# RG-LRU gates as 64x64 blocks between the steps of a later projection, in a stage with a written order

## The chip, the cores and the metric

The kernel runs on one core of a Trainium2 chip. The metric is the device time of one execution in microseconds. The core has a matrix engine (TensorE, PE in the profile; PEld is its loading of weights), two engines for element-wise work (VectorE = DVE, ScalarE = ACT), GpSimd (POOL), and SyncE (SP), which here issues all transfers. TensorE writes to eight banks of PSUM, of 512 float32 values per partition each; VectorE and ScalarE read them.

## What is computed

One layer of a diffusion backbone in float32: 1024 latent tokens and 256 context tokens of width 1024 are normalised, modulated, and sent through a mixer and a feed-forward part. The part that matters here is the first half of the mixer:

```
h      = modulate(rms_norm(x), sh1, sc1)
xr, gr, cq, ckv, kr = split(h @ w_in)            # 512 + 512 + 256 + 128 + 32 columns
xc     = depthwise_conv4(xr)                     # along the tokens
r      = sigmoid(block_diag(w_a) xc + b_a)       # 8 heads of 64x64, two directions
i      = sigmoid(block_diag(w_x) xc + b_x)
log_a  = -8 r softplus(-lambda)
u      = sqrt(1 - exp(2 log_a)) * (i * xc)
h_t    = a_t h_(t-1) + u_t                       # forward and backward, context first
y_lru  = (h_fwd + h_bwd) * gelu(gr)
x      = x + gt1 * rms_norm([y_lru, attention(cq, ckv, kr)] @ w_out)
```

The modulation vectors are `silu(c) @ w_mod + b_mod`, six pieces of 1024. Pieces 0 and 1 (sh1, sc1) are needed before the mixer; 3 and 4 (sh2, sc2) after it, in the layout of the features; 2 and 5 (gt1, gt2), the residual gates, as rows.

## The kernel before

Tokens are worked on in 10 tiles of 128 (two of context, eight latent). Matmuls on float32 data go in three terms: every operand is split into a high part and the rest (`split`, lines 78 to 80: a copy on ScalarE or GpSimd, then a subtraction, line 76, on VectorE or GpSimd).

The first stage (to line 466) normalises and transposes the tokens, modulates them (`h_mod`, line 214; its affine is lines 188 to 192), and makes the 416 token-major columns of the projection (`tok_mm`, line 275, 24 matmuls a tile; `tok_out`, line 288). This stage stands inside `tc.manual_schedule()`, which means that each engine, the issuing of transfers on SyncE included, runs its instructions in the order in which the code creates them. It ends at line 466.

The second stage (lines 500 to 679) is ordered by the planner of the language. It makes the eight blocks of 128 feature-major columns (`proj`, line 485). A block is 8 steps k, and a step is three terms (lines 492, 494, 496) for three chunks of 512, 512 and 256 tokens (blocks m = 0 to 3, the recurrent ones) or two of 512 (m = 4 to 7, the gelu ones). The weights come by `load_w` and `prep_w`. After a recurrent block comes `conv` (lines 532 to 537: two reads on ScalarE, six multiply-adds on VectorE). A block's gates (`gate`, line 540) are four products, for two directions and two gates, each with a 128x128 matrix that holds two 64x64 heads on its diagonal and zeros beside them, in plain float32, three chunks each. Sigmoid (line 545), exponential and tanh (`coefs`, lines 565 and 566), and root (line 573) follow on ScalarE, the rest and the scans on VectorE (lines 567 to 591). The planner loads a new function table on ScalarE whenever the function's set changes (ACT_TABLE_LOAD).

Between the projections the later modulation runs as 16 steps (`mod2_step`, line 413): each brings two slices of 512 KB and makes four matmuls on four column tiles (line 424). After four steps the sum is copied and either transposed (line 433) or, for the residual gates, summed into a row (line 436), worked on in four halves (lines 439 to 445) and written to memory, from where `gt_row` spreads it later.

`tok_norm` (line 610) normalises the token-major columns, with a square root on ScalarE inside `rstd_of` (line 102). `ckv_t` (line 631) transposes the key latents in three pieces. Then the attention's operands are made (from line 688), and from line 968 the attention runs in a written order.

Pages come from pools: `R` has 12 pages, `W` five. In the second stage PSUM holds two "big" tiles of three banks and two small ones of one bank ("sm").

Of the kernel before, what the change touches and what calls it, by code (L numbers as in the profile page):

```python
# [34 lines left out]
def hybrid_layer_kernel(ctx: ExitStack, tc: tile.TileContext, A, out):  # L35
# [87 lines left out]
    for h in range(2):  # L123
        V.tensor_tensor(sel2[:, h:h + 1], ident[:, 64 * h:64 * h + 1], ident[:, 64 * h + 32:64 * h + 33], ALU.add)

# [277 lines left out]

    def mod2_load(s):

        n, kp = divmod(s, 4)
        col = (2, 1, 0, 3)[n]
        w2[s] = R(), R()
        for j in range(2):
            k = 2 * kp + j  # L410
            nc.sync.dma_start(out=w2[s][j][:, :D], in_=A["w_mod"][k * 128:(k + 1) * 128, col * 1024:(col + 1) * 1024])

    def mod2_step(s):

        n, kp = divmod(s, 4)
        if s + 1 < 16:
            mod2_load(s + 1)
        if kp == 0:
            acc2[n] = ps_small()
# [6 lines left out]
        if kp == 3:  # L426
            mr = R()
            S.activation(mr[:, 0:512], acc2.pop(n), AF.Copy)
            po = ps_small()
            if n < 2:  # L430
                pt = po[:, 0:8].rearrange("p (m h) -> p m h", h=2)
                for m in range(4):
                    T.matmul(pt[:, m, :], mr[:, m * 128:(m + 1) * 128], sel2, start=True, stop=True)
                V.tensor_copy(mod2[:, n].rearrange("p (h m) -> p m h", h=2), pt)
            else:
                T.matmul(po[0:2, :], sel2, mr[:, 0:512], start=True, stop=True)
                r = 2 * (n - 2)
                rw, gr = (mr[0:2, 512 + 256 * x:768 + 256 * x] for x in range(2))
                for h in range(2):
                    c = slice(h * 256, (h + 1) * 256)  # L440
                    for x, q_ in ((rw, r), (gr, r + 1)):
                        nc.sync.dma_start(out=x, in_=A["rows"][q_:q_ + 1, :].rearrange("o (a b) -> (o a) b", a=2)[:, c])
                    V.tensor_tensor(rw, po[0:2, c], rw, ALU.add)
                    V.tensor_tensor(rw, rw, gr, ALU.mult)
                    nc.sync.dma_start(out=gt_d[n - 2:n - 1, :].rearrange("o (a b) -> (o a) b", a=2)[:, c], in_=rw)
# [5 lines left out]

    for g in range(2, 5):
        if g == 2:
            last_x = load_x(9)
# [30 lines left out]
    def proj(w, chunks, name):  # L485
# [3 lines left out]
        for k in range(8):  # L489
# [10 lines left out]
    nl, sp, z, z2, q = (C([128, 8]) for _ in range(5))  # L500
    V.tensor_scalar(out=nl, in0=P("lam"), scalar1=-1.0, scalar2=None, op0=ALU.mult)
    V.tensor_tensor(z, nl, P("lam"), ALU.max)
    S.activation(z, z, AF.Exp, scale=-1.0)
    V.tensor_scalar(out=sp, in0=z, scalar1=2.0, scalar2=None, op0=ALU.add)
    V.reciprocal(out=sp, in_=sp)
    V.tensor_tensor(z, z, sp, ALU.mult)
    V.tensor_tensor(z2, z, z, ALU.mult)
    V.tensor_scalar(out=q, in0=z2, scalar1=1.0 / 15, scalar2=None, op0=ALU.mult)
    for d in (13, 11, 9, 7, 5, 3):
        V.scalar_tensor_tensor(out=q, in0=q, scalar=1.0 / d, in1=z2, op0=ALU.add, op1=ALU.mult)  # L510
    V.scalar_tensor_tensor(out=q, in0=q, scalar=1.0, in1=z, op0=ALU.add, op1=ALU.mult)
    V.tensor_scalar(out=nl, in0=nl, scalar1=0.0, scalar2=None, op0=ALU.max)
    V.scalar_tensor_tensor(out=sp, in0=q, scalar=2.0, in1=nl, op0=ALU.mult, op1=ALU.add)
    n8, p4 = (C([128, 8]) for _ in range(2))
# [1240 lines left out]
```

## Time and profile before

| | us |
|---|---|
| median of three runs | 1337.65 (1335.8 to 1337.68) |
| the profiled execution | 1337.59 |
| its span, first to last instruction | 1335.7 |
| TensorE busy | 1279.3 (96%) |
| VectorE busy | 1059.3 (79%) |
| ScalarE busy | 730.3 (55%) |
| GpSimd busy | 524.3 (39%) |

The rows below are of four kinds. A row of stretches gives the busy time of each engine in a window, the granted TensorE clock (1.00 is full) and what the transfers moved. A row in order of time gives the start, the duration of the merged run, the engine, the line, the operation, what it writes and reads, the shapes, the count, and in brackets the idle time before it and who ended it. Names like `pf`, `pg`, `pm`, `ck` are the program's tiles without their numbers. A float32 matmul outside the three-term scheme shows as two instructions.

### The profile page before, as it was taken

To read this page: it belongs to the slowest core of one execution; us is meant where nothing else is said; L and a number is where in the kernel's file an instruction comes from. 1 tells how busy PE (TensorE), PEld (TensorE's weight loads), DVE (VectorE), ACT (ScalarE), POOL (GpSimd) and SP (SyncE) were. 2 spreads that over 40 slices of the span, in tenths; PEclk is the share of its full clock that TensorE was granted. 3 is DMA by queue.
4 is the path that set the end of the run, shared out by engine and by line. 5 is a ranking of instruction groups with operands and counts; after the bars stand their busy time and mean duration, and the time that the engine had idled before them with its cause. 6 is when DMAs were issued, how large, how long until landed. Compare 5 with 4: busy or idle time off the path is not lost. (4 is left out here: it accounts for less than half of the span.)

```text
span 1335.7 us, 18049 instructions
## 1 busy us (share of the span) xinstructions
PE 1279.3 (96%) x6490; PEld 1049.6 (79%) x6490; DVE 1059.3 (79%) x1633; ACT 730.3 (55%) x1366; POOL 524.3 (39%) x441
## 2 busy tenths in 40 slices
PE   5999999799999999999998999999999999999895
PEld 3796666687999999888776888888888888878684
DVE  3654677768898988847589888887778779998998
ACT  4533785458999999934355433344334435334362
POOL 2410000215666666723042344423442324873922
PEclk8999999899999999999998999999999999999998
DMA  9533244000000001333321222222222368031033
GB/s 372 197 111 127 86 143 130 12 1 1 1 1 1 1 1 49 111 126 140 129 95 48 95 95 86 72 79 95 91 68 78 111 204 316 1 110 64 16 137 115
DMA packets 42184, 124.21 MB, mean 93 GB/s; under 512 B 4696, under 2 KB 4976, under 8 KB 42096
## 3 DMA queue, kind: packets, MB, share of 16 engines
q1 hardware_dynamic: 42096, 123.07, 26.2%
q8 instruction: 51, 0.84, 0.3%
q14 instruction: 37, 0.30, 0.1%
HBM read 101.02 MB, written 22.03 MB: 92 GB/s over the span
## 5 line engine op out<-in xcount | busy, mean ns | idle before, releaser
L1217 PE MATMUL b<-l,f 128*128 128x512 f32 x620 | 242.6, 391 | 5.6 <-DVE f L76 5.6
L1216 PE MATMUL b<-l,f 128*128 128x512 f32 x620 | 242.9, 392 | 3.9 <-DVE l L76 3.8
L1215 PE MATMUL b<-l,f 128*128 128x512 f32 x620 | 242.4, 391 | 0.5 <-issue 0.5
L1217 PEld LDWEIGHTS b<-l,f 128*128 128x128 f32 x620 | 117.0, 189 | 30.7 <-DVE f L76 6.4
L1216 PEld LDWEIGHTS b<-l,f 128*128 128x128 f32 x620 | 116.9, 189 | 30.5 <-DVE l L76 6.5
L906 POOL TENSOR_SCALAR r<-r,c 128x512 f32<-128x512 f32 (+1 forms) x128 | 100.9, 800 | 97.2 <-DVE c L901 68.2
L1215 PEld LDWEIGHTS b<-l,f 128*128 128x128 f32 x620 | 117.0, 189 | 25.2 <-issue 0.7
L1190 ACT ACTIVATE f<-w 128x1024 fp32r<-128x1024 f32 x21 | 22.3, 1060 | 198.8 <-POOL w L1187 198.8
L883 DVE TENSOR_REDUCE c<-s 128x1 f32<-128x512 f32 (+1 forms) x192 | 108.6, 594 | 25.6 <-PE s L880 24.1
L76 DVE TENSOR_TENSOR f<-w,f 128x1024 fp32r<-128x1024 f32 (+1 forms) x89 | 97.1, 1093 | 33.9 <-ACT f L1190 32.9
L1274 DVE SCALAR_TENSOR_TENSOR l<-f,c,l 128x1023 f32<-128x1023 f32 x88 | 123.4, 1403 | 0.7
L894 ACT ACTIVATE r<-s,c 128x512 f32<-128x512 f32 (+1 forms) x192 | 117.5, 620 | 6.2 <-DVE c L901 4.7
L1184 POOL TENSOR_TENSOR w<-w 128x512 f32<-128x512 f32 x21 | 27.9, 1328 | 230.7 <-DVE f L76 230.7
L76 DVE TENSOR_TENSOR l<-t,l 128x512 fp32r<-128x512 f32 x128 | 81.5, 678 | 1.4 <-ACT l L69 1.2
L914 PE MATMUL t<-c,r 128*128 128x128 f32 x640 | 81.7, 273 | 0.9 <-DVE r L76 0.6
L69 ACT ACTIVATE l<-t 128x512 fp32r<-128x512 f32 x128 | 69.4, 595 | 8.5 <-PE t L914 7.7
L1268 ACT ACTIVATE l<-f,c 128x1024 f32<-128x1024 f32 x44 | 54.5, 1238 | 34.9 <-DVE f L1255 34.4
L914 PEld LDWEIGHTS t<-c,r 128*128 128x128 f32 x640 | 71.3, 140 | 2.6 <-PE t L914 0.8
L878 PE MATMUL s<-r,w 96*128 96x512 f32 (+1 forms) x192 | 69.5, 362 | 1.0 <-ACT r L894 0.7
L1063 PE MATMUL po<-l,r 128*128 128x512 f32 x256 | 69.3, 390 | 0.0
L938 PE MATMUL o<-l,r 128*128 128x256 f32 x256 | 68.7, 301 | 0.0
L879 PE MATMUL s<-r,w 96*128 96x512 f32 (+1 forms) x192 | 68.6, 358 | 0.0
(376 smaller groups left out, 3318.2 us busy)
## 6 DMA issues: line engine op xcount, KB each, us to landing
w<-in_w_up SPq DMA_DIRECT2D x44, 512.0 KB
r<-in_w_mod SPq DMA_DIRECT2D x32, 512.0 KB
act<-l SPq DMA_DIRECT2D x22, 512.0 KB
l<-in_w_m SPq DMA_DIRECT2D x16, 512.0 KB
l<-act SPq DMA_DIRECT2D x30, 256.0 KB
l<-in_w_dn SPq DMA_DIRECT2D x30, 256.0 KB
w<-in_w_fm SPq DMA_DIRECT2D x8, 512.0 KB
w<-in_w_out SPq DMA_DIRECT2D x8, 512.0 KB
```

The source lines that it names most:

```text
L69: S.activation(o, i, AF.Copy)
L76: return (V if e == "v" else G).tensor_tensor(o, src, f(hi), ALU.subtract)
L878: T.matmul(ps[:, :n], qh[0:96, q], kh[0:96, a:a + n], start=True, stop=False)
L883: V.tensor_reduce(out=stat[:, i % 4, c:c + 1], in_=sc[i, c][:, :CK[c][1]], op=ALU.min, axis=AX.X)
L894: S.activation(pt_[i][:, a:a + n], sc.pop((i, c))[:, :n], AF.Exp, scale=-1.0, bias=st[:, 3:4], accum_out=st[:, 4 + c:5 + c])
L906: G.tensor_scalar(out=p[:, a:a + n], in0=p[:, a:a + n], scalar1=stat[:, i % 4, 7:8], scalar2=1.0, op0=ALU.mult, op1=ALU.mult)
L914: T.transpose(ps[:, c, :], pt_[i][:, (c0 + c) * 128:(c0 + c + 1) * 128], ident)
L1063: T.matmul(po[:, n * 512:(n + 1) * 512], w, wo[k][0][:, n * 512:(n + 1) * 512], start=st, stop=en)
L1215: T.matmul(po, wh, bh, start=k == 0 and b == wb[0][1], stop=False)
L1216: T.matmul(po, wh, bl, start=False, stop=False)
L1217: T.matmul(po, wl, bh, start=False, stop=k == 3 and b == wb[-1][1])
L1274: V.scalar_tensor_tensor(out=x[:, a], in0=x0[:, b], scalar=P("fcw", j * 3 + k, 1), in1=x[:, a], op0=ALU.mult, op1=ALU.add)
```

## The change

- The gates become 64x64 blocks. For a block m, a direction d and a chunk c, `gate_group` makes four matmuls with their own quadrants of the array: the two heads of gate a on the diagonal quadrants, reading `xc`, and the two heads of gate x on the other two, writing each other's half of the partitions. For gate x a copy of `xc` with its halves exchanged is made by two transfers (`xcs`). Each group fills two small banks and is followed by two sigmoids.
- The six groups of a block stand between the steps k = 0 to 5 of a later projection: `of` says that the third projection (m=2) carries block 0, the fourth (m=4) block 1, the fifth (m=3) block 2 and the seventh (m=6) block 3. The first two projections carry the eight modulation steps that are left.
- The written order now reaches to the end of this stage.
- The residual gates' vectors are summed on VectorE: 16 steps (`gt_step`), each one load of 512 KB and one multiply-add of 128x1024, most of them in the first stage; at the end of each half, two matmuls add the two halves' partitions to a row.
- `tok_norm` stands before the fifth projection, `ckv_t` after the sixth. From the third projection on the weights' high parts are copied on GpSimd. The constants of the decay are made at the start. Gate weights come as four transfers a block.

```diff
+    def gt_step(s, psum):
+        n, k = divmod(s, 8)
+        if s + 2 < 16:
+            gt_load(s + 2)
+        c = sil[:, 2 * k:2 * k + 1]
+        r = gw.pop(s)[:, :D]
+        if k == 0:
+            gacc[n] = r
+            V.tensor_scalar(out=r, in0=r, scalar1=c, scalar2=1.0, op0=ALU.mult, op1=ALU.mult)
+        else:
+            V.scalar_tensor_tensor(out=gacc[n], in0=r, scalar=c, in1=gacc[n], op0=ALU.mult, op1=ALU.add)
...
+        if k == 7:
+            po = psum()
+            for h in range(2):
+                T.matmul(po[0:2, :], e01[:, 2 * h:2 * h + 2], gacc[n][:, h * 512:(h + 1) * 512], start=h == 0, stop=h == 1)
+            rw, gr = (grow[n][0:2, x * 512:(x + 1) * 512] for x in range(2))
+            V.tensor_tensor(rw, po[0:2, :], rw, ALU.add)
+            V.tensor_tensor(rw, rw, gr, ALU.mult)
+            nc.sync.dma_start(out=gt_d[n:n + 1, :].rearrange("o (a b) -> (o a) b", a=2), in_=rw)
...
+    GT = (range(0, 2), range(2, 4), range(4, 6), range(6, 9), range(9, 11), range(11, 14))
     for g in range(2, 5):
...
         tok_mm(2 * g, range(8))
         tok_out(2 * g)
         if g < 4:
-            last_h = h_mod(g + 1)
+            h_mod(g + 1)
+        for s_ in GT[2 * (g - 2)]:
+            gt_step(s_, bank0)
         tok_mm(2 * g + 1, range(8))
         tok_out(2 * g + 1)
-    tc_ms.close()
+        for s_ in GT[2 * (g - 2) + 1]:
+            gt_step(s_, bank0)
...
+            for x in between.get(k, ()):
+                x()
         return po
...
+        y = xcs[m] = R()
+        for p in (0, 64):
+            nc.sync.dma_start(out=y[64 - p:128 - p, :], in_=x[p:p + 64, :])
...
+    def gate_group(m, d, c):
+        if c == 0:
+            RI[m, d] = R(), R()
+        po = [ps_g() for g in range(2)]
+        a, n = CH3[c]
+        for h in (0, 64):
+            for g in range(2):
+                o = h ^ (64 * g)
+                T.matmul(po[g][o:o + 64, 0:n], wg[m][h:h + 64, d, g, :], (xcs if g else xc)[m][h:h + 64, a:a + n], start=True, stop=True,
+                         tile_position=(h, o))
+        for g in range(2):
+            S.activation(RI[m, d][g][:, a:a + n], po[g][:, 0:n], AF.Sigmoid, bias=P("bx" if g else "ba", d * 4 + m, 1))
...
-    order = list(range(8))
-    after = {1: 0, 2: 1, 3: 2, 5: 3}
+    order = (0, 1, 2, 4, 3, 5, 6, 7)
+    of = {2: 0, 3: 1, 4: 2, 6: 3}
     ws = prep_w(load_w(A["w_fm"][0]), "a", "v")
     raw = load_w(A["w_fm"][1])
...
+    mod2_load(0)
     for n, m in enumerate(order):
-        po = proj(ws, CH3 if m < 4 else CH3[:2], f"pf{m}")
+        if m < 4:
+            load_wg(m)
+        if n == 4:
+            tok_norm()
+        g = of.get(n)
+        if g is not None:
+            btw = {k: [lambda k=k: gate_group(g, k // 3, k % 3)] for k in range(6)}
+        elif n < 2:
+            btw = {2 * k + 1: [lambda k=k: mod2_step(4 * n + k)] for k in range(4)}
+        else:
+            btw = {}
+        po = proj(ws, CH3 if m < 4 else CH3[:2], f"pf{m}", btw)
         if n < 7:
-            ws = prep_w(raw, "a", "v")
+            ws = prep_w(raw, "g" if 1 < n else "a", "v")
             if n < 6:
                 raw = load_w(A["w_fm"][order[n + 2]])
-        for s_ in STEPS2[n]:
-            mod2_step(s_)
+        if g is not None:
+            au = coefs(g)
         if m < 4:
-            load_wg(m)
             conv(m, po)
         else:
-            gated(m - 4, po)
-        if m in after:
-            au = coefs(after[m], gates(after[m]))
-            if m == 5:
-                tok_norm()
-            scans(after[m], au)
-        if m == 6:
+            gelu(m - 4, po)
+        if g is not None:
+            roots(au)
+            scans(g, au)
+        if m >= 4:
+            gated(m - 4)
+        if n == 0:
+            for s_ in (14, 15):
+                gt_step(s_, ps_g)
+        if n == 5:
             ckv_t()
+        if n == 6:
             raw = load_w(A["w_ukv"])
             wkh, wkl = prep_w(raw, "a", "v")
+    tc_ms.close()
```

## Rows read from the trace of the kernel before

**Rows 1.** Stretches: us, busy (count) of PE, PEld, DVE, ACT, POOL, clock, DMA share, GB/s
```profile
90.75:251.90 161.15, 160.81 (x733) 107.55 (x732) 100.58 (x129) 94.59 (x85) 8.74 (x5) 1.00 0.35 116
...
258.80:293.00 34.20, 32.79 (x179) 29.42 (x180) 25.23 (x38) 18.70 (x35) 6.66 (x9) 0.92 0.00 1
```

**Rows 2.** TensorE in order of time: start, us, what, [idle before, releaser]
```profile
258.81 0.69 PE L637 MATMUL ck<-c,l 128*128 128x128 f32 x2 [6.88 <-DVE l L642]
```

**Rows 3.** VectorE in order of time, at the end of the stage
```profile
240.07 2.89 DVE L578 SCALAR_TENSOR_TENSOR r<-r,r 128x1280 f32<-128x1280 f32 x2 [7.53 <-ACT r L573]
...
262.39 1.28 DVE L702 SCALAR_TENSOR_TENSOR l<-pb,c,l 128x1024 fp32r<-128x1024 f32 x1 [0.32 <-ACT l L701]
```

**Rows 4.** TensorE in order of time: the starts of two steps, three and two chunks
```profile
90.75 0.75 PE L492 MATMUL pf<-l,w 128*128 128x512 f32 x3
...
92.52 0.75 PE L492 MATMUL pf<-l,w 128*128 128x512 f32 x3
...
207.73 0.62 PE L492 MATMUL pf<-l,w 128*128 128x512 f32 x2
...
209.09 0.62 PE L492 MATMUL pf<-l,w 128*128 128x512 f32 x2
```

**Rows 5.** TensorE in order of time: a modulation step, two gates, a row sum
```profile
121.90 1.06 PE L424 MATMUL pm<-r,c 128*32 128x512 f32 x8
122.90 1.12 PE L543 MATMUL pg<-r,l 128*128 128x512 f32 x2
...
132.39 4.56 PE L543 MATMUL pg<-r,l 128*128 128x512 f32 x12
136.60 0.93 PE L492 MATMUL pf<-l,w 128*128 128x512 f32 x3
...
182.04 1.02 PE L436 MATMUL pm<-r,c 128*2 128x512 f32 x2
```

**Rows 6.** ScalarE in order of time, in the first stage
```profile
77.35 0.52 ACT L292 ACTIVATE l<-po 128x416 f32<-128x416 f32 x1 [3.99 <-PE po L286]
...
78.61 1.91 ACT L190 ACTIVATE l<-q,c,c 128x256 f32<-128x256 f32 x4
```

**Rows 7.** VectorE's last split of the first stage, and TensorE's tile 8
```profile
80.34 3.72 DVE L76 TENSOR_TENSOR l<-l,l 128x512 fp32r<-128x512 f32 x4 [3.58 <-POOL l L73]
...
81.69 0.35 PE L284 MATMUL po<-r,l 128*128 128x416 f32 x1
```

**Rows 8.** VectorE in order of time: convolution, multiply-adds, a scan of one block
```profile
126.10 4.85 DVE L537 SCALAR_TENSOR_TENSOR r<-r,c,r 128x1022 f32<-128x1022 f32 x6 [0.68 <-ACT r L533]
...
147.38 2.89 DVE L578 SCALAR_TENSOR_TENSOR r<-r,r 128x1280 f32<-128x1280 f32 x2 [7.53 <-ACT r L573]
...
154.18 2.33 DVE L582 TENSOR_TENSOR_SCAN r<-r,r 128x1024 f32<-128x1024 f32 x1
```

**Rows 9.** Stretches: transfers at their fastest in this stage
```profile
200.00:202.00 2.00, 2.00 (x10) 1.67 (x9) 0.00 (x0) 1.99 (x2) 0.00 (x0) 1.00 0.97 313
```

**Rows 10.** ScalarE in order of time: reads, table loads and functions of one block
```profile
124.64 1.42 ACT L533 ACTIVATE r<-pf,c 128x1280 f32<-128x1280 f32 x1
126.08 1.28 ACT L545 ACT_TABLE_LOAD   x1
127.38 1.33 ACT L545 ACTIVATE r<-pg,c 128x1280 f32<-128x1280 f32 x1
...
139.64 2.62 ACT L565 ACTIVATE r<-r,c 128x1280 f32<-128x1280 f32 x2
...
146.07 2.44 ACT L573 ACTIVATE r<-r 128x1280 f32<-128x1280 f32 x2
```

**Rows 11.** Stretches: the clock during and after the wait of rows 2
```profile
254.00:256.00 2.00, 0.00 (x0) 0.00 (x0) 2.00 (x2) 0.00 (x0) 0.00 (x0) 0.50 0.00 0
...
262.00:264.00 2.00, 2.00 (x8) 1.75 (x7) 1.35 (x2) 1.36 (x2) 0.00 (x0) 0.50 0.00 0
```

**Rows 12.** The first of the decay's constants: duration, first and last start
```profile
L501 DVE TENSOR_SCALAR c<-c x1: 171/171/171, 3.0 to 3.0; 128x8 f32<-128x8 f32 x1
```

More of the change, by code (lines that the diff above doesn't have):

```diff
@@ L402, in hybrid_layer_kernel, with gt_load @@
     acc2 = {}
+    e01 = C([128, 4])
+    V.memset(e01, 0.0)
+    V.memset(e01[:, 0:1], 1.0)
+    V.memset(e01[:, 3:4], 1.0)
+    gw, gacc, grow = {}, {}, {}
+    def gt_load(s):
+        n, k = divmod(s, 8)
+        gw[s] = R()
+        col = (0, 3)[n]
+        nc.sync.dma_start(out=gw[s][:, :D], in_=A["w_mod"][k * 128:(k + 1) * 128, col * 1024:(col + 1) * 1024])
+    def gt_step(s, psum):
+        n, k = divmod(s, 8)
+        if s + 2 < 16:
[7 more added lines that the diff above has]
+            V.scalar_tensor_tensor(out=gacc[n], in0=r, scalar=c, in1=gacc[n], op0=ALU.mult, op1=ALU.add)
+        if k == 6:
+            grow[n] = R()
+            for x in range(2):
+                nc.sync.dma_start(out=grow[n][0:2, x * 512:(x + 1) * 512],
+                                  in_=A["rows"][2 * n + x:2 * n + x + 1, :].rearrange("o (a b) -> (o a) b", a=2))
+        if k == 7:
[6 more added lines that the diff above has]
+            nc.sync.dma_start(out=gt_d[n:n + 1, :].rearrange("o (a b) -> (o a) b", a=2), in_=rw)
+    w2 = {}
+    acc2 = {}
     def mod2_load(s):
         n, kp = divmod(s, 4)
-        col = (2, 1, 0, 3)[n]
+        col = (2, 1)[n]
         w2[s] = R(), R()
@@ L415, in mod2_step @@
         n, kp = divmod(s, 4)
[L416 removed]
+        if s + 1 < 8:
             mod2_load(s + 1)
         if kp == 0:
[L419 removed]
+            acc2[n] = ps_g()
         ws_ = w2.pop(s)
@@ L428, in mod2_step @@
             S.activation(mr[:, 0:512], acc2.pop(n), AF.Copy)
[L429 to L445, printed above, removed]
+            pt = ps_g()[:, 0:8].rearrange("p (m h) -> p m h", h=2)
+            for m in range(4):
+                T.matmul(pt[:, m, :], mr[:, m * 128:(m + 1) * 128], sel2, start=True, stop=True)
+            V.tensor_copy(mod2[:, n].rearrange("p (h m) -> p m h", h=2), pt)
     def gt_row(n, page):
@@ L483, in prep_w, with proj @@
         return hi, lw
-    def proj(w, chunks, name):
+    def proj(w, chunks, name, between={}):
         hi, lw = w
@@ L538, in conv, with ps_g, gelu, gated @@
                                        op0=ALU.mult, op1=ALU.add)
-    def gate(m, d, g):
-        po = ps1.tile([128, 1536], F32, tag="big", name=f"pg{m}{d}{g}", bufs=2)
-        for a, n in CH3:
-            T.matmul(po[:, a:a + n], wg[m][:, d * 2 + g, :], xc[m][:, a:a + n], start=True, stop=True)
-        r = R()
-        S.activation(r, po[:, 0:NTOK], AF.Sigmoid, bias=P("bx" if g else "ba", d * 4 + m, 1))
-        return r
-    ysum = {}
-    def gated(m, po):
-        g = R()
-        S.activation(g[:, :SEQ], po[:, :SEQ], AF.Gelu_apprx_tanh)
-        V.tensor_tensor(ysum[m], ysum[m], g[:, :SEQ], ALU.mult)
-    def gates(m):
-        return [(gate(m, d, 0), gate(m, d, 1)) for d in range(2)]
-    def coefs(m, ri):
+        y = xcs[m] = R()
+        for p in (0, 64):
+            nc.sync.dma_start(out=y[64 - p:128 - p, :], in_=x[p:p + 64, :])
+    def ps_g():
+        cnt[0] += 1
+        return ps1.tile([128, 512], F32, tag="g", name=f"pm{cnt[0]}", bufs=2)
+    RI = {}
+    def gate_group(m, d, c):
[8 more added lines that the diff above has]
+                         tile_position=(h, o))
+        for g in range(2):
+            S.activation(RI[m, d][g][:, a:a + n], po[g][:, 0:n], AF.Sigmoid, bias=P("bx" if g else "ba", d * 4 + m, 1))
+    ysum = {}
+    gel = {}
+    def gelu(m, po):
+        gel[m] = R()
+        S.activation(gel[m][:, :SEQ], po[:, :SEQ], AF.Gelu_apprx_tanh)
+    def gated(m):
+        V.tensor_tensor(ysum[m], ysum[m], gel.pop(m)[:, :SEQ], ALU.mult)
+    def coefs(m):
         au = []
         for d in range(2):
-            r, i = ri[d]
+            r, i = RI.pop((m, d))
             c = slice(d * 4 + m, d * 4 + m + 1)
@@ L569, in coefs, with roots, scans @@
         return au
-    def scans(m, au):
+    def roots(au):
         for a, b, h in au:
             S.activation(b, b, AF.Sqrt)
+    def scans(m, au):
         hs = []
```

58 lines of the change are left out of this document (30 added, 28 removed).

## The prediction

> **What bounds the kernel now.** I read the table of stretches first. From 90.75 to 251.90, the projections of the mixer, TensorE is busy 160.81 of 161.15 us [rows 1]. So TensorE's own work is the length of that stretch, and ScalarE (94.59) and VectorE (100.58) have slack. Then TensorE stands still for 6.88 us, until the last transposes of the key latents get a bank from VectorE [rows 2]. The reason is in VectorE's order of time: the chain of the last channel block runs from 240.07 on, and the first instruction of the next stage that is free of it starts at 262.39 [rows 3]. From there to 293 the attention is prepared [rows 1], and the attention and all behind it is the same code. So what moves the moment 262.39 moves the end by as much.
>
> **TensorE's work in the stage.** A step k of a projection takes 1.77 us with three chunks and 1.36 us with two [rows 4], so the eight projections are 4 x 8 x 1.77 + 4 x 8 x 1.36 = 100.1 us, before and after. Two of the old gates took 136.60 - 132.39 = 4.21 us, so all 16 took 33.7 us [rows 5]. The new gates are 24 groups of four 64x64 matmuls. The nearest row is a step of the later modulation: four matmuls on four column tiles, 512 columns each, took 122.90 - 121.90 = 1.00 us [rows 5], so four tiles ran beside each other there. I take 1.0, 1.0 and 0.57 us (256 columns, an estimate from the 1.0) for the three chunks, 8 x 2.57 = 20.6 us. The bounds are 17 us, if nothing is lost between kinds of matmuls (half of the old columns), and 41 us, if a group's tiles run two by two; I stay with the row that is like it. Eight of 16 modulation steps leave TensorE, eight stay (7.8 us). The two old sums for the gate rows (1.02 us each [rows 5]) become two sums of two matmuls, 3.6 us. With some 3 us of transposes that stay, the new work is 100.1 + 20.6 + 7.8 + 3.6 + 3 = 135 us against 161: TensorE alone would gain 26 us.
>
> **What the fixed order costs.** Every engine now issues this stage as the code is written. That a queue doesn't let a ready instruction pass a waiting one is shown by the part that was already fixed: ScalarE stood 3.99 us before L292 at 77.35, and L190, whose transposes were long done, came behind it at 78.61 [rows 6]. So I went through the new code, engine by engine, with the durations of the rows, and looked for the places where TensorE meets a wait. There are six.
>
> First, the row sum at gate step 7. TensorE has it between the token projections of tiles 7 and 8, which it reaches at 81.69 [rows 7]. VectorE ends the last split before it at 80.34 + 3.72 = 84.06 [rows 7], and then the code gives it steps 4 to 7, each one multiply-add of 128x1024. From the 128x1280 one (2.89 for two, 1.40 each [rows 8]) that is 1.15 each, and the load of step 7 has to wait for a page, so it is ready at 89.4: 7.5 us of waiting. Behind it stand tiles 8 and 9, and behind those the stage. Steps 0 to 3 before that are free: VectorE has 3.58 us idle there [rows 7], and the weight splits that were done early in this stretch move away.
>
> Second, the first weights. SyncE issues in code order too: the load of the first projection's weights stands behind 16 loads of 512 KB for the gate vectors, the last of which wait for pages that VectorE frees step by step, and behind the store of the first gate row. I get its issue at about 101 and, at 313 GB/s [rows 9] with three loads ahead, its landing at 105 to 106.5, then a copy on ScalarE. The projection starts at 107.9 instead of 90.75: 7.5 and 5 us of waits, 1.8 us for the sum, and 2.6 us for the clock (below).
>
> Third, the second row sum stands behind the first projection, and on VectorE steps 14 and 15 stand behind its convolution. That needs the two ScalarE reads of the finished sum (2.5 us, the second alone 1.42 [rows 10]), six VectorE instructions (4.85 [rows 8]) and two steps (2.3): TensorE waits 9.7 us. The planner's old order had modulation steps there.
>
> Fourth, the gates of block 1. A group takes both small banks, so the next group waits for two sigmoids. When the projection of m=4 starts, ScalarE still has the second half of two exponentials and two tanh, two reads (2.5), a table load and two roots, then a table load back (1.28 each, 2.62 for a pair of exponentials, as much for tanh, 2.44 for the roots [rows 10]): 11 us, then 1.0 for the first two sigmoids (1.33 for 1280 columns [rows 10], 0.52 for 512), against 3.7 us until TensorE wants the second group. Wait: 8.6 us.
>
> Fifth, the gates of block 2, the dearest. In front of that projection stands the token norm, whose square root is on ScalarE and whose input comes from VectorE. There it stands behind the whole scan chain of block 1 (2.8 for two multiply-adds, 2.8 for two products of that size, 4.5 for two scans of 1024 [rows 8], 1.2 each for the scans of 256 and the sum, estimated by length), which starts when the roots end, 10.5 us after the projection of m=4. ScalarE can't take the sigmoids that stand behind the root. TensorE stops before the second group for 21.6 us.
>
> Sixth, the transposes of the key latents after m=5 want three small banks and there are two. The third waits for a VectorE read that stands behind the scans of block 2 and a gating product: 14.7 us. This is the wait of [rows 2] moved, not removed.
>
> Two short waits of 0.8 us for a copy before the modulation's transposes come to these. The sum of waits is 7.5 + 5.0 + 9.7 + 8.6 + 21.6 + 14.7 + 1.6 = 68.7 us.
>
> **The clock.** [...] Six waits of 5 us and more make 15.6 us. The lower bound is nothing, where the next wait swallows it.
>
> **The tail.** After the last projection the new order still has block 3: the scans start 9.5 us after the end of the projection of m=6 and take 11.3 us, and the sum, two products and the split of the next weights 4.6 us. The first free VectorE instruction comes 14.4 us after TensorE's last projection; before it was 10.5 us (262.39 - 251.9). So 4 us more.
>
> **The sum.** 26.2 off, 68.7 + 15.6 + 4 on: 62 us. The profiled execution took 1337.59 us (its span 1335.7), 0.06 below the median of three, 1337.65, so the time is 1337.6 + 62 = 1400 us.
>
> **What is free.** The constants of the decay move to the front; the first of them already ran at 3.0 us [rows 12], so nothing changes. The weight copies move to GpSimd, which was idle 152 of the 161 us [rows 1], and their results are needed a projection later; they can slow VectorE, by 0 to 3 us. The swapped copy of each convolution (two transfers of 320 KB) is needed a projection later, and the four smaller gate-weight loads cost SyncE 0.4 us each in a queue that by then has room.
>
> [...] No row shows row tiles: those of [rows 5] are column tiles that share one bank. In a group here the blocks at rows 0 and 64 of one gate write different partitions of one bank. [...]
>
> **Rivals.** One: the blocks of a group run in two rounds, for the shared bank. Then 20.6 becomes 41.2 us; the waits for ScalarE shrink by 2, and the time is 1400 + 18.5 = 1418. Against it: four tiles on one bank did run beside each other [rows 5]. Chance 0.15.
>
> Two: the waits stand, but less is lost around them: the clock's 15.6 us fall into the next waits, and the planner, which still places the instructions behind the stage, puts 5 us of them ahead of the last scans. Then 62 - 20.6 gives 1379. Chance 0.15.
>
> Three, the other side: ScalarE and VectorE do keep up, because a group's sigmoids are taken before the backlog in front of them, and TensorE meets no long wait. The place is the second group of each gated projection and the third key transpose. The price is the 26 us of work less 4 of the tail: 1337.6 - 22 = 1315. It decides when all waits of the stage together stay below 22 us. For it speaks that both engines have 60 us of slack [rows 1]; against it that the slack isn't where the waits are, and [rows 6]. Chance 0.08.
>
> **How the numbers follow.** The forecast of 1400 has 0.6, with 1388 to 1412 for what the estimates of single durations leave open. The rest is rival one 0.15, two 0.15, three 0.08, and 0.02 for waits that happen to cancel the gain. A measurement of this kernel can tell about 0.2% from no change: faster 0.08, same 0.02, slower 0.90. The range goes from 1366 (rival two with another 13 us of waits gone) to 1424 (rival one and 6 us of contention on VectorE).
>
> **What would show it.** In the changed kernel's order of time TensorE should stop before the first row sum (waiting for VectorE, 5 to 9 us), before the first projection, before the second row sum, before the second gate group of the projections of m=4 and m=3 (waiting for ScalarE, 8 and 20 us), and before the third key transposes. The granted clock should show 0.5 after each. Gates should fall from 33.7 to about 20 us. The first scores, at 293 now, should start near 355. If the stage has less than 22 us of idle TensorE, the prediction is wrong in sign; if a group takes 2 us instead of 1, rival one holds.

## The result, and the profile after

The changed kernel takes 1418.09 us (median of four runs, 1417.03 to 1418.69), the kernel before 1337.54 (four runs): a ratio of 1.0605 [1.0586, 1.0623], 80.5 us slower. The profiled execution of the changed kernel took 1417.03 us, its span is 1415.2. TensorE is busy 1275.2 us, nearly as long as before (1279.3); what grew is the time in which it stands still.

First the six largest entries of the list of TensorE's waits in the changed kernel from 81 to 372 us (line, for whom; total, how often, the longest):

```profile
PE pm L604 <- ACT r L607: 31.2, 2, 23.1
PE pm L701 <- DVE l L706: 17.0, 1, 17.0
PE pb L787 <- DVE w L76: 10.5, 1, 10.5
PE pm L456 <- DVE r L447: 10.3, 1, 10.3
PE q L456 <- DVE r L447: 8.6, 1, 8.6
PE pf L546 <- ACT w L69: 8.0, 1, 8.0
```

Six waits stand in front of the very instructions that the prediction named: the two row sums (L456), the first projection (L546), two gate groups (L604, twice) and the key transposes (L701). The seventh, L787, lies behind the last projection. Each of the rest is 1.5 us or less.

TensorE in order of time shows the two long gate waits, and how long a gate group takes when nothing is waited for:

```profile
173.87 1.09 PE L604 MATMUL pm<-r,l 64*64 64x512 f32 x8
174.89 0.85 PE L546 MATMUL pf<-l,w 128*128 128x512 f32 x3
...
176.82 1.09 PE L604 MATMUL pm<-r,l 64*64 64x512 f32 x8
...
179.77 0.66 PE L604 MATMUL pm<-r,l 64*64 64x256 f32 x8
180.37 0.85 PE L546 MATMUL pf<-l,w 128*128 128x512 f32 x3
...
204.71 2.56 PE L604 MATMUL pm<-r,l 64*64 64x512 f32 x8 [8.13 <-ACT r L607]
...
222.29 1.09 PE L604 MATMUL pm<-r,l 64*64 64x512 f32 x8
...
248.37 2.55 PE L604 MATMUL pm<-r,l 64*64 64x512 f32 x8 [23.06 <-ACT r L607]
...
295.59 0.69 PE L701 MATMUL pm<-c,l 128*128 128x128 f32 x2 [16.95 <-DVE l L706]
```

Four blocks of 512 columns take 1.02 us (173.87 to 174.89) and of 256 columns 0.60. A step with a group in it takes 2.95 us (173.87 to 176.82); 1.77 of step [rows 4] and 1.02 of group leave 0.16 us for the two switches of kind.

Why TensorE stopped for 23.06 us is read from the two queues that feed it, ScalarE first, then VectorE, in the same stretch:

```profile
228.95 2.43 ACT L635 ACTIVATE r<-r 128x1280 f32<-128x1280 f32 x2
244.92 0.21 ACT L102 ACTIVATE rs<-rs 128x10 f32<-128x10 f32 x1 [13.54 <-DVE rs L101]
...
247.63 1.26 ACT L607 ACTIVATE r<-pm,c 128x512 f32<-128x512 f32 x2
```

```profile
230.25 1.49 DVE L642 SCALAR_TENSOR_TENSOR r<-r,r 128x1280 f32<-128x1280 f32 x1 [8.68 <-ACT r L635]
...
244.72 0.17 DVE L101 TENSOR_SCALAR rs<-c 128x10 f32<-128x10 f32 x1
```

The sigmoids (L607) stand behind the token norm's square root (L102), which stands behind VectorE's whole scan chain of block 1 (230.25 to 244.72). ScalarE is idle for 13.54 us, and the values that it should read have long been there: TensorE made the first group of block 2 at 222.29.

The stretches (busy PE, granted clock, transfers): the whole of the two stages from tile 8 on, then the times after the six waits.

```profile
81.80:326.84 245.04, 166.41 (x819) 0.83 0.28 90
90.00:93.00 3.00, 2.61 (x4) 0.50 0.57 171
110.00:116.00 6.00, 5.15 (x14) 0.50 1.05 361
144.00:147.00 3.00, 2.42 (x3) 0.50 0.59 153
204.00:209.00 5.00, 4.29 (x12) 0.50 0.54 131
248.00:253.00 5.00, 4.63 (x14) 0.50 0.00 0
295.00:301.00 6.00, 5.41 (x17) 0.50 0.21 74
```

In the kernel before, the same work (tile 8 to the end of the projections) is this row:

```profile
81.69:251.90 170.21, 169.88 (x781) 1.00 0.34 113
```

So the stretch grew by 245.04 - 170.21 = 74.8 us. TensorE's idle time went from 0.3 to 78.6 us. In the six windows 24.5 us of work ran at half the clock, which lost 12.3 us (the windows leave out the ends of these stretches; read in steps of 0.5 us the loss is 13.5). And TensorE's work at full clock fell from 169.9 to 166.4 - 12.3 = 154.1, that is by 15.8 us (17.0 with the 13.5): 78.3 + 12.3 - 15.8 = 74.8. This is a sum of times, not of causes: a term that shrinks can come back in another. The rest is the tail:

```profile
342.49 2.47 DVE L775 SCALAR_TENSOR_TENSOR l<-pb,c,l 128x1024 fp32r<-128x1024 f32 x2
```

The instruction that stood at 262.39 [rows 3] now stands at 342.49, 80.1 us later: 74.9 up to the end of TensorE's projections, 5.2 behind it.

### The profile page after: what moved, and what is told of

The parts are those of the page before. It is cut to its first block, busy times and chain, and to the rows that moved or that the text cites. A ratio compares the mean times of both kernels' runs of the same rounds, so it can differ in the third digit from the quotient of the medians.

```text
span 1415.2 us, 18181 instructions
## 1 busy us (share of the span) xinstructions
PE 1275.2 (90%) x6526; PEld 1037.9 (73%) x6526; DVE 1081.0 (76%) x1648; ACT 731.8 (52%) x1392; POOL 527.1 (37%) x446
## 5 line engine op out<-in xcount | busy, mean ns | idle before, releaser
L956 DVE TENSOR_REDUCE c<-s 128x1 f32<-128x512 f32 (+1 forms) x192 | 108.8, 595 | 26.0 <-PE s L953 24.5
L73 POOL TENSOR_SCALAR w<-w 128x1024 fp32r<-128x1024 f32 x5 | 6.0, 1207 | 197.4 <-DMA w<-in_w_fm 134.7
L951 PE MATMUL s<-r,w 96*128 96x512 f32 (+1 forms) x192 | 69.5, 362 | 1.0 <-ACT r L967 0.7
```

The lines of the kernel that those rows point to most:

```text
L951: T.matmul(ps[:, :n], qh[0:96, q], kh[0:96, a:a + n], start=True, stop=False)
L956: V.tensor_reduce(out=stat[:, i % 4, c:c + 1], in_=sc[i, c][:, :CK[c][1]], op=ALU.min, axis=AX.X)
```

## The experiments

Theory: the time is lost because each engine runs this stage as it is written, and a ready instruction stands behind a waiting one. Rivals: the blocks themselves are dear (they share banks, they need copies); the work moved to VectorE makes that engine the bound. A time without an interval is of one execution; the four of the changed kernel lie within 1.7 us.

### One wait at a time

The token norm earlier:

```diff
-        if n == 4:
+        if n == 1:
             tok_norm()
```

> The changed kernel with the token norm moved from ahead of the fifth projection to ahead of the second one; the order stays fixed. Theory (ScalarE's queue: the sigmoids of block 2 stand behind the norm's square root, which stands behind VectorE's scans): the 23.1 us wait before the second gate group of block 2 shrinks to that of block 1 before it, 8 to 9 us, because the backlog of exponentials, reads and roots is the same; time 1418 - 15 = 1403 us (1399 to 1407). Rival one (the wait is for the gates' own inputs, the swapped copy or the banks): it stays at 23 us, time within 3 us of 1418. Rival two (the norm was all of it): the wait goes, 1418 - 25 = 1393 us.

1401.23 us, 16.9 less. TensorE's wait before block 2's second group went from 23.06 us to 8.11, as long as block 1's 8.13:

```profile
232.26 2.55 PE L604 MATMUL pm<-r,l 64*64 64x512 f32 x8 [8.11 <-ACT r L607]
```

The theory holds: moving the norm, with its two short roots on ScalarE, took off what it predicted. The backlog of exponentials, reads and roots that stands in front of every block's sigmoids is left.

The first weights earlier (behind the transposes of tiles 8 and 9, and the split ahead of tile 8):

```diff
+        if g == 3:
+            raw0, raw = W(), W()
+            nc.sync.dma_start(out=raw0, in_=A["w_fm"][0])
+            nc.sync.dma_start(out=raw, in_=A["w_fm"][1])
+        if g == 4:
+            ws = W(F32R), W(F32R)
+            split(raw0, ws[0], ws[1], "a", "v")
...
-    ws = prep_w(load_w(A["w_fm"][0]), "a", "v")
-    raw = load_w(A["w_fm"][1])
```

> The changed kernel with the loads of the first two projections' weights ahead of the later gate-vector loads on SyncE, and the first split ahead of tile 8. Theory (SyncE's queue): the first projection starts right behind tile 9, near 102.7 us instead of 110.85, without a drop of the clock; the row sums wait as before (8.6 and 10 us); the first modulation step then waits some 2 us for its page. Time 1418 - 8 = 1410 us (1407 to 1413). Rival (the transfers bound this stretch, whatever their order): the modulation steps wait for what the projection gained, time within 2 us of 1418.

1413.65 us, 4.4 less where 8 were expected. The 8.0 us wait is gone, but the first modulation step now waits 4.45 us for its page (2 were expected) and takes 3.12 us, where it took 1.06 in the changed kernel (at 117.30); from these two I estimate that the clock falls there instead:

```profile
111.02 3.12 PE L485 MATMUL pm<-r,c 128*32 128x512 f32 x8 [4.45 <-DMA r<-in_w_mod]
```

About half of the gain was taken by the wait for the next transfer.

The row sums later (`gt_sum` is the part of `gt_step` at k == 7; the first stands behind tile 9, the second behind the first projection, with steps 14 and 15 ahead of that):

```diff
             gt_step(s_, bank0)
+    gt_sum(0, bank0)
     pe_ctx.close()
...
+        if n == 0:
+            for s_ in (14, 15):
+                gt_step(s_, ps_g)
         po = proj(ws, CH3 if m < 4 else CH3[:2], f"pf{m}", btw)
...
         if n == 0:
-            for s_ in (14, 15):
-                gt_step(s_, ps_g)
+            gt_sum(1, ps_g)
```

> The changed kernel with the first row sum behind tile 9, and gate steps 14 and 15 ahead of the first projection in the code instead of behind its convolution; loads as in the changed kernel. Theory (each wait hides the next: the first projection's weights come at the same time whatever TensorE did before): the 8.6 us before the first sum go, but the wait before the first projection grows from 8 to 17 to 19 us, so nothing is gained there; the 10.3 us before the second sum go, and some 5 us of waiting for modulation pages come in the second projection. Time 1418 - 7 = 1411 us (1405 to 1414). Rival (the waits add up, each with its clock): 1418 - 19 - 4.5 = 1395 us.

1408.49 us, 9.6 less. Both waits before the sums went (8.6 and 10.3 us), but two others grew:

```profile
107.13 1.44 PE L548 MATMUL pf<-l,w 128*128 128x512 f32 x3 [14.00 <-ACT w L69]
...
147.93 3.17 PE L486 MATMUL pm<-r,c 128*32 128x512 f32 x8 [7.79 <-DMA r<-in_w_mod]
```

Of 18.9 us of waits, 12.8 came back in front of the weights (6.0 more) and the modulation pages (6.8 more). So the first wait cost little, because the second stood behind it anyway.

### All of them at once

Five repairs in one kernel (these three, the key transposes behind the second projection, the split of the key and value weights ahead of block 3's chain):

> The changed kernel with five repairs at once, order still fixed: the token norm ahead of the second projection, the first two weights' loads early, both row sums late (as in the three runs on single repairs), the transposes of the key latents behind the second projection instead of behind the sixth, and the split of the key and value weights ahead of the last block's chain. Theory (in a fixed order a wait that is taken away brings the next one up): some 10 us before the first modulation step and 6 us before a later one for their pages, 9 and 9 us for sigmoids, and a new wait of 14 us in the seventh projection, whose low weights are split by VectorE behind the scans of block 2; time 1418 - 20 = 1398 us (1390 to 1405). Rival (the repairs add up: 16.9, 4.4 and 9.6 us as measured, and the 17.0 and 10.5 us waits with 2.3 of clock): 1418 - 61 = 1357 us.

1391.11 us, 27 less, where the three single runs and the two other waits add up to 61. A new wait is the longest now, the seventh projection's low weights, split by VectorE behind the scans of block 2:

```profile
PE pm L687 <- ACT r L690: 16.2, 2, 8.1
PE pf L647 <- DVE w L76: 15.2, 1, 15.2
PE pb L835 <- DVE l L824: 8.9, 1, 8.9
PE pf L643 <- DVE r L459: 8.3, 1, 8.3
```

The waits for sigmoids and the new one are of the size expected; the 8.3 us (the first projection's banks, behind the row operations of the first sum) were not. The wait behind the last projection is still 8.9 us, though the split that it was for now comes early: another VectorE instruction ends it. Here, in a written order, the waits were repaired one behind the other and did not add up.

### The order given back to the planner

```diff
             gt_step(s_, bank0)
+    tc_ms.close()
     pe_ctx.close()
...
             wkh, wkl = prep_w(raw, "a", "v")
-    tc_ms.close()
     pe_ctx.close()
```

> The changed kernel with the fixed order ended where it ended before the change, ahead of the projections; gates as 64x64 blocks, their place in the code, the modulation vectors on VectorE and the order of the blocks stay. Theory (the fixed order of the projection stage costs, the new work does not): TensorE's waits of that stage fall from about 79 us to under 25 us (the first row sum's 8.6 us lies in the part that was fixed before and stays), and the time is 1318 to 1350 us. Rival (the blocks, or the work moved to VectorE, cost by themselves): long waits stay, time above 1385 us. Third: the planner pulls the four matmuls of a group apart, so that gates cost 2 us a group; then 24 us more than the theory's time.

1385.46 us, a ratio to the kernel before of 1.0359 [1.0342, 1.0377]. Only 33 of the 80 us come back, and my theory (1318 to 1350) was wrong. TensorE's idle time up to the end of the projections fell from 78.6 to 28.7 us (under 25 expected) and no wait is over 8.8 us, but other things are dearer. To see whether it is the blocks, they went alone into the kernel before, whose order is planned (the edit below, with `gate_group`, the swapped copies and the four gate-weight loads a block):

```diff
-        return [(gate(m, d, 0), gate(m, d, 1)) for d in range(2)]
+        for d in range(2):
+            for c in range(3):
+                gate_group(m, d, c)
+        return [RI.pop((m, d)) for d in range(2)]
```

> One part of the change alone: the kernel before, its order still planned, with the gates as 64x64 blocks on four quadrants (with the swapped copy of the convolution and two small banks for a group); modulation, order of the blocks and all else as before. If the blocks bring what TensorE's rows say, gates fall from 33.7 us to 21 and the first score and the end come 13 us earlier: 1325 us (1322 to 1329). Rival (each block's six groups can't run ahead of their sigmoids, with two banks for all of them, and the planner mixes sigmoids and exponentials as in the run with the order planned, which doubled those table loads): the gates' chain into VectorE becomes longer than what TensorE gains, 1342 to 1360 us, and ScalarE shows 8 table loads for the sigmoid instead of 4.

1393.45 us, 1.0429 [1.0411, 1.0447]: the blocks, with what comes along with them, cost 56 us here, more than the rival allowed (1342 to 1360, with 8 table loads for the sigmoid). More than the blocks changed: a gate of the kernel before wrote a big tile of three banks and had one sigmoid of 1280 columns [rows 10], a group writes two small banks and has a sigmoid for each chunk. TensorE of that kernel, in order of time, then its gates by line (busy time, mean ns), the gates of the kernel before by line, and ScalarE's table loads in the kernel with the blocks:

```profile
190.49 1.08 PE L563 MATMUL pm<-r,l 64*64 64x512 f32 x4
192.35 1.08 PE L563 MATMUL pm<-r,l 64*64 64x512 f32 x4 [0.79 <-ACT r L566]
```

```profile
L563 PE MATMUL pm<-r,l 64*64 64x512 f32 (+1 forms) x192 | 44.5, 572 | 18.3 <-ACT r L566 18.0
```

```profile
L543 PE MATMUL pg<-r,l 128*128 128x512 f32 (+1 forms) x96 | 38.0, 535 | 0.0
```

```profile
L566 ACT ACT_TABLE_LOAD x12 | 15.4, 1283 | 1.2 <-PE pm L563 0.8 <-DVE r L602 0.2
L588 ACT ACT_TABLE_LOAD x8 | 10.3, 1283 | 0.1
L596 ACT ACT_TABLE_LOAD x8 | 10.3, 1283 | 0.1
```

The planner issues half a group (x4, two blocks) and then waits for a sigmoid. A half takes 1.08 us, and a whole group of x8 took 1.09 above: here the blocks saved time only where all four stood together. The gates are 44.5 us of TensorE (a half took 1.97 us at 207.01; the granted clock is 0.93 in the mean from 81.80 to 290), where the same count gives 38.0 for the full gates of the kernel before and 26.6 for the changed kernel. The sigmoid's table is loaded 12 times, where the kernel before and the changed one load it four times; with those of the exponentials and roots that is 20 us more on ScalarE. In the run before this one the modulation steps were torn in the same way (15.8 us for 64 instructions, 9.6 in the changed kernel). Up to the end of the projections TensorE's idle time is 25.9 us longer than in the kernel before, its work at full clock some 13, and about 9, an estimate from the rows that took about twice their usual time, go to the lower clock; 7 come behind that. So under this planner, with two small banks, the blocks cost time, and the order written here costs more than it saves. Whether full gates in two small banks would have cost as much under the planner was not run.

### What the blocks are worth

Each row tile into its own bank:

```diff
-                T.matmul(po[g][o:o + 64, 0:n], wg[m][h:h + 64, d, g, :], (xcs if g else xc)[m][h:h + 64, a:a + n], start=True, stop=True,
+                T.matmul(po[h // 64][o:o + 64, 0:n], wg[m][h:h + 64, d, g, :], (xcs if g else xc)[m][h:h + 64, a:a + n], start=True, stop=True,
```

> The changed kernel with the results of a gate group sorted otherwise into its two banks: what the rows 0 to 63 of the array produce goes into one bank and what the rows 64 to 127 produce into the other, so that no bank is written from two row tiles. (The sigmoids then read halves of both gates, so the gate values are not those of the reference; the work is the same.) If row tiles can't write one bank at the same time, a group here takes less than in the changed kernel, where 512 columns took 1.02 us and 256 took 0.60, and the time falls by up to half of 21 us. Theory (four blocks ran beside each other already): 1.02 and 0.60 us as before, time 1418 within 2 us.

1417.2 us, and a group is no shorter:

```profile
173.27 1.09 PE L604 MATMUL pm<-r,l 64*64 64x512 f32 x8
174.29 0.85 PE L546 MATMUL pf<-l,w 128*128 128x512 f32 x3
```

1.02 us, as with the shared bank. Full gates in the changed kernel's order (the swapped copies go with the blocks, and one load of gate weights a block stands for four):

```diff
-        for h in (0, 64):
-            for g in range(2):
-                o = h ^ (64 * g)
-                T.matmul(po[g][o:o + 64, 0:n], wg[m][h:h + 64, d, g, :], (xcs if g else xc)[m][h:h + 64, a:a + n], start=True, stop=True,
-                         tile_position=(h, o))
+        for g in range(2):
+            T.matmul(po[g][:, 0:n], wg[m][:, d * 2 + g, :], xc[m][:, a:a + n], start=True, stop=True)
```

> The changed kernel with its fixed order, but the gates as full 128x128 matmuls (two for a group in place of four blocks, with no swapped copy); all else as in the changed kernel. This prices the blocks inside the fixed order. Theory: a group of 512 columns takes some 1.75 us instead of 1.02 and one of 256 some 0.9 instead of 0.6, 24 groups together 14 us more; the second groups of blocks 1 and 2 wait for ScalarE anyway, which hides 2 to 3 of it: 1418 + 11.5 = 1430 us (1426 to 1433). Rival (the waits hide the gates, or the blocks run one after another): 1416 to 1420 us.

1418.77 us, 1.0615 [1.0598, 1.0633] of the kernel before, where the changed kernel has 1.0605: no difference, and the rival's time was right. A step with a full group takes 3.47 us against 2.95, so the gates are 9 us longer. But the first gate group stands at 170.11 instead of 173.87, and the key transposes end their wait at 295.14 instead of 295.59:

```profile
170.11 1.88 PE L591 MATMUL pm<-r,l 128*128 128x512 f32 x4
...
173.58 1.88 PE L591 MATMUL pm<-r,l 128*128 128x512 f32 x4
...
295.14 0.69 PE L687 MATMUL pm<-c,l 128*128 128x128 f32 x2 [16.84 <-DVE l L692]
```

The waits end when ScalarE and VectorE say so, and part of what TensorE does between them is hidden. The 3.8 us before the first group come from the first two projections: there TensorE's rows are back at their usual length sooner, which gains 1.4 us (the projection starts at 110.79 instead of 110.85, the first modulation step at 115.82 instead of 117.30), and waits of 1.0 us for modulation pages and 0.8 for a split are missing. With the blocks SyncE issues four gate-weight loads a block (4.36 us for the first four) ahead of those pages, here one; that this is the cause was not tried.

From the start of the first projection to the end of the last one, the changed kernel and then the one with full gates:

```profile
110.85:326.84 215.99, 153.96 (x766) 0.84 0.23 72
```

```profile
110.79:327.32 216.53, 157.83 (x671) 0.86 0.18 63
```

Idle time fell from 62.0 to 58.7 us. The loss to the lower clock, read in steps of 0.5 us, fell from 12.2 to 8.2: behind four of the five waits in this stretch the lower clock lasted 2 to 3 us less, behind the wait for the second sum 1.5 us more. TensorE's work at full clock grew by 7.8. So the waits hide 3.3 of the 7.8 us, and 4.0 are made up by the clock; the stretch got 0.5 us longer. Why the clock rose sooner with full gates no run here shows.

### A new order

Each group, coefficient, root, scan, gate-vector step, load and split of the changed kernel got its own place between the projections' steps, chosen with the durations of its rows. A part of the plan, for the third and fourth projections (n, and the step k that it follows; `gate m d c`, `prep` a split, `wl` a load of weights, `wg` one of gate weights):

```diff
+        (2, 3): 'coef 0 0 / gt 15',
+        (2, 4): 'coef 0 1 / wg 3',
+        (2, 5): 'wg 1 / sum 1',
+        (2, 6): 'roots 0',
+        (2, 7): 'wl ukv / prep 3 g / scans 0',
+        (2, 8): 'gate 1 1 0',
+        (3, 1): 'gate 1 1 1',
+        (3, 2): 'wl 4 / gate 1 0 0',
+        (3, 3): 'gate 1 0 2',
...
```

> The same instructions as in the changed kernel, with blocks, in a fixed order that was worked out anew with the durations of its rows: each gate group, coefficient, root, scan, gate-vector step, load and split has its own place between the projection's steps, so that no wait of TensorE should be over 3 us. Theory (the order alone cost the 80 us): TensorE's waits in the stage 13 to 20 us in all, none over 3 us, no granted clock of 0.5 in the stage, time 1339 us (1332 to 1350). Rival (the new work costs by itself, on VectorE and ScalarE, whatever its order): long waits in other places, time above 1360 us.

1351.43 us, 1.0108 [1.0092, 1.0123]. The order takes back 66.7 of the 80.5 us; besides it only three weight copies changed places between ScalarE and GpSimd. TensorE's waits from 81 to 300 us:

```profile
PE pb L845 <- DVE l L834: 12.7, 1, 12.7
PE q L457 <- DVE r L447: 4.8, 1, 4.8
PE pf L657 <- DVE w L76: 3.8, 2, 3.5
```

TensorE's idle time up to the end of the projections is 14.1 us, within the 13 to 20 expected. But two waits of the stage are over 3 us (4.8 and 3.5), and the clock fell to 0.50 behind both, from 91 to 97 and from 188 to 196 us, which lost 3.0 and 3.8 us: the sum took 3.57 us there and 1.88 in a run below where it didn't wait. The 12.7 us lie behind the projections. The time is 12 us over my 1339 and just above my range (1332 to 1350). Against the kernel before, the first projection starts 9.9 us later (100.61 against 90.75 [rows 4]), the projections end 8.0 later (259.86 against 251.90), and the first free VectorE instruction comes 13.5 later (275.88 against 262.39 [rows 3]).

The same order with full gates:

> The kernel of the new fixed order with full 128x128 gates in place of the 64x64 blocks (no swapped copies); all else the same. It prices the blocks where TensorE is not kept waiting. By the rows a group of 512 columns costs 0.5 us more and one of 256 0.1 us more, 9 us in all. Theory (TensorE sets most of that order): 6 to 9 us slower than with the blocks. Rival (ScalarE and VectorE set the pace, as in the run with full gates in the changed kernel): within 2 us of it.

1351.81 us, 1.0112 [1.0095, 1.0129]: no difference again, where the theory had 6 to 9 us. The projections take 159.7 us in place of 159.3. TensorE's work at full clock is 5.2 us more in them, its idle time 3.2 less (6.1 and 9.3) and the clock's loss 1.5 less (2.2 and 3.7). The blocks save less here than in the changed kernel; two groups at least are torn, because the swapped copy comes late for them. Behind the projections both wait for the same VectorE chain (12.7 us).

Two more runs look at what is left of the 14 us. GpSimd's splits of the query weights, which run beside the last block's chain, on other engines:

```diff
-        split(raw, h_, l_, "g", "g")
+        split(raw, h_, l_, "a", "v")
```

> The kernel of the new fixed order with the four splits of the query weights, which GpSimd does between 250 and 260 us beside the last block's chain, on ScalarE and VectorE instead. In the reordered kernel VectorE's instructions in those 10 us took 1.84 to 3.12 us where their like takes 1.22 to 1.49 elsewhere, 5.4 us more in all. Theory (VectorE and GpSimd slow each other): products of 128x1280 take 1.49 us there and sums of 128x1024 take 1.22, the last scans start 2 to 4 us earlier, and of that 1.7 us go back for the two subtractions: 1351.4 - 2 = 1349.5 us (1347.5 to 1351.5). Rival (the long instructions have another cause, such as reads of PSUM or transfers): they stay above 1.8 us and the time does not fall.

1348.32 us, 1.0086 [1.0069, 1.0102]. VectorE in the reordered kernel, then GpSimd in it, then VectorE without the splits:

```profile
253.63 2.87 DVE L711 TENSOR_TENSOR l<-l,r 128x1024 f32<-128x1024 f32 x1
...
258.46 3.12 DVE L733 SCALAR_TENSOR_TENSOR r<-r,r 128x1280 f32<-128x1280 f32 x1
```

```profile
252.72 2.70 POOL L76 TENSOR_TENSOR l<-l,l 128x768 fp32r<-128x768 f32 x1
```

```profile
253.13 1.21 DVE L711 TENSOR_TENSOR l<-l,r 128x1024 f32<-128x1024 f32 x1
...
255.67 1.48 DVE L733 SCALAR_TENSOR_TENSOR r<-r,r 128x1280 f32<-128x1280 f32 x1
```

2.87 and 3.12 us became 1.21 and 1.48, and the chain of the last scans (L733) starts 2.8 us earlier. The theory holds; the intervals of the two ratios overlap a little, the rows don't.

And VectorE's added work, with 12 of its 16 multiply-adds left out:

> The kernel of the new fixed order with 12 of the 16 multiply-adds for the gate vectors left out (their loads stay; the gate vectors are then sums of a quarter of their terms, so the outputs differ). It prices VectorE's added work. Theory (with the order mended, VectorE's added 20 us lie in its gaps; only the first row sum waits for them, 4.84 us and 2.3 of clock): 1351.4 - 7 = 1344 us (1342 to 1346). Rival one (VectorE is the bound of the whole stage): most of the 15.4 us come off, 1336 to 1340 us. Rival two (nothing of it is on the path): 1350 to 1352 us.

1345.54 us, 1.0057 [1.0042, 1.0073], 5.9 less. In the profiled execution, the fastest of the four (1342.91), the sum stands at 85.39 without a wait and the first projection at 91.86. The rival by which VectorE bounds the whole stage (1336 to 1340) falls: 15.4 us of work were taken away and 5.9 came off the time. If the two savings of 3.1 and 5.9 us add up, which was not tried, 5 of the 14 us stay open.

## Why the prediction was right, and where its terms were off

**The mechanism** was right, place by place. The six waits, predicted and measured: 7.5 and 8.59 before the first sum, 5.0 and 8.00 before the first projection, 9.7 and 10.32 before the second sum, 8.6 and 8.13 in block 1, 21.6 and 23.06 in block 2, 14.7 and 16.95 before the key transposes. The sum of the waits was 68.7; the idle time is 78.3 more than before. Four of the six are long by 0.6 to 2.3 us. For the two row sums, sizes explain half of the first and all of the second: VectorE's multiply-adds take 1.28 us each (I had 1.15 from another row) and its six convolution instructions 5.35 (4.85). The other two I did not take apart. The first projection's wait is 3 us longer though its weights' load was issued at 101.1, as predicted: it landed at 109.7 and not by 106.5. VectorE waited for gate-vector pages there too, 2.32 and 2.91 us from 97 and 100.6 us on.

**TensorE's work** was the term most off: 26.2 us were to come off, 15.8 to 17.0 did. The gates came out as predicted (8 x 2.64 = 21.1 against 20.6). But I added up the new work from its parts (135) and took it from the measured total of the old one (161), whose parts add up to 155 only. The 6 us that were missing I put down to the switches between kinds of matmul, and these are in the new stage too: 32 inserted groups and steps at the 0.16 us that a step left above are 5 us, an estimate. The rest of the difference I can't assign.

**The clock** lost 12.3 to 13.5 us in six places (15.6 predicted). The 15.6 are six times 2.6 us, half of the 5.2 from 258.81 [rows 2] to 264 at a clock of 0.50 [rows 11]. That every wait of 5 us and more costs as much was an estimate that no run shows: in the six windows above the work at 0.50 was 2.42 to 5.41 us, which lost 1.2 to 2.7 us each. **The tail** is 5.2 us (4 predicted). The first scores start at 371.6 us, where the prediction had about 355.

**What the sum hid.** It counted the shorter gates as 13 us won on the path. The runs with full gates show, in two orders, that they were worth nothing on the whole: TensorE waits for other engines or a transfer, and part of the time that it saves between the waits is given back at the next one. The other part is lost to the lower clock, which cost more with the blocks (12.2 us against 8.2 in the first order, 3.7 against 2.2 in the second); why is not shown. The time was still predicted about right, because the waits had been worked out with the short gates. So the forecast was 18 us low for the sizes of terms (10 of work, 10 of waits, 1 of the tail, less 3 of the clock), and with six waits in their places no mechanism of that size was missing.

**What was luck.** The measured 1418 lies 6 us above the 1388 to 1412 that were given with the forecast itself. The wide range, 1366 to 1424, holds it only because its upper end was that of rival one with contention on top, and rival one's mechanism isn't there.

**The rivals.** Rival one gave the time that was measured, 1418, by a mechanism that isn't there: a group takes 1.02 us and not 2, with one bank or two, and a single block takes as long (last section). This is measured for two row tiles that write different partitions of a bank; other forms were not run. Rival two (1379) fell with the time. Whether each drop of the clock lengthened the whole or only shortened the next wait, no run separates. Rival three (the engines keep up) fell with 78.6 us of idle time against the 22 from which it would have held; the new order shows how far one other order brings it, 1351 us.

**What was called free.** The four gate-weight loads cost SyncE 0.66 to 1.11 us each (4.36 us for the first block's four), not 0.4. The weight copies on GpSimd were put at 0 to 3 us for VectorE, and that is the size that the run without GpSimd's splits showed for four others (3.1 us). No version of the changed kernel that was run beats the kernel before.

## What to carry to other kernels

An order written out by hand has to be checked engine by engine, and each queue behind each wait: a square root of 0.21 us, with its norm, cost 17 us by its place here. Ask which engine ends the waits before shortening another one's work: TensorE's shorter gates were worth nothing on the whole, for waits that ScalarE and VectorE end grew by part of what they saved (3.3 of 7.8 us in the changed kernel's order), and more work at the lower clock took 4.0. Waits in one chain don't add up when they are repaired: five repairs whose parts add up to 61 us brought 27.

## What the hardware showed that I had not expected

One 64x64 block alone, or two, take as long as four (1.07 us for x2, 1.08 for x4, 1.09 for x8). The single one is from the reordered kernel, where the other three of its group wait for the swapped copy:

```profile
227.94 1.07 PE L697 MATMUL pm<-r,l 64*64 64x512 f32 x2
```

In these runs the gain showed only where the matmuls of all four quadrants stood directly behind each other.

VectorE was held up by GpSimd: a sum of two tiles of 128x1024 took 2.87 us beside GpSimd's subtraction and 1.21 without it. GpSimd's began at 252.72 and took 2.70, so it ended at 255.42; VectorE's ended at 256.50, 1.1 us behind that, about its own length. A GpSimd copy, which reads one tile, was enough too: in the run without the splits a product of 128x1280 that began at 249.75, beside a copy from 249.05 to 250.73, took 2.33 us, and 1.48 at 254.27 with none beside it. By what mechanism the one holds up the other no run here shows.
